# A written-out issue order around the third and fourth head pairs of an attention block: w_out's first half loaded earlier, its folds spread, w_ada's last quarters moved behind the fourth pair's scores

## The chip, the cores and the metric

One Trainium2 chip, one core. The metric is the device time of one execution in microseconds (us); lower is better. The kernel computes one layer of a decoder trunk for 512 tokens of width 1024 in float32.

## The reference, cut to what matters

```python
mod = silu(c) @ w_ada[l] + b_ada[l]                  # 1 x 6144: shift, scale, gate, twice
sh_m, sc_m, gt_m, sh_f, sc_f, gt_f = split(mod, 6)
u = layer_norm(x) * (1.0 + sc_m) + sh_m
proj = u @ w_in                                      # q, k, v, forget gate, xb, gb
attn = forgetting_attention(q, k, v, f_logit + b_f)  # 8 heads x 64, blocks of 128 queries
lru  = rg_lru_branch(xb, gb, ...)                    # 512 channels
mix  = concat([rms_norm(attn, g_attn), rms_norm(lru, g_lru)]) @ w_out
x = layer_norm(ALPHA * x + (1.0 + gt_m) * mix, ln1_g, ln1_b)
u = layer_norm(x) * (1.0 + sc_f) + sh_f
ffn = hierarchical_moe(u, ...)                       # top-1 of 4 groups, top-2 of 4 experts
x = layer_norm(ALPHA * x + (1.0 + gt_f) * ffn, ln2_g, ln2_b)
```

## The kernel before, in words

Float32 products of the large matrices are made from three passes of a short-mantissa type: each operand is split into a high part (a cast on ScalarE, `whi`) and the rest (a subtraction on VectorE, `wlo`), and `mm3` (lines 101 to 103) issues high x high, high x low and low x high. Weights arrive by DMA as raw 512 KB tiles in five buffers of a pool (`raw`, `NRW = 5` on line 219); their split halves have four buffers of each kind (`hilo`, `NHL = 4`). A tile that is asked for takes a buffer that an earlier tile has left, and the DMA that fills it waits, in SyncE's queue, until the last reader of that earlier tile is done. SyncE issues all these transfers in one order, so a transfer that waits holds up all behind it. Matmul results live in eight PSUM banks (`ps`); small working tiles of 2 KB per partition (`t2k`: softmax rows `pr`, their transposes `pt`, sums `part`) have ten buffers.

The work comes in a front part (conditioning, LayerNorm, projections, the RG-LRU branch), a middle part (attention, the output projection, the router's folds) and a last part (LayerNorm, routing, sixteen experts, the final LayerNorm). In the middle part the order of every engine is written by hand: `TAIL` (line 39) returns a list of steps, and line 1580 calls them in turn. On SyncE, TensorE, ScalarE, VectorE and GpSimd the instructions run in exactly that order (line 1072). The steps that matter here:

- `pj(i, n)` (line 1097) projects the queries (n = 0) or the keys (n = 1) of head pair i: 24 matmuls on TensorE, then `qk_evac` (line 662), one operation on ScalarE and one on VectorE. It also calls `w_ahead`, which loads a coming block of `w_in` and splits it; a separate step `w_ahead` stands once in the list.
- `AL` (line 1111) loads one quarter of a 512-column block of `w_ada` (one 512 KB transfer on SyncE). `AC` (line 1115) multiplies it with the conditioning vector on TensorE: every second `AC` issues the eight matmuls of two quarters (line 290), and the fourth of a block has ScalarE copy the sum out and issue a small DMA. `AU[j]` (line 1066) uses the finished block j: eight small matmuls (line 318 or 512) and one VectorE or ScalarE operation.
- `S[m]`, `N[m]`, `T[m]`, `PV[m]` (`att_S`, `att_N`, `att_T`, `att_PV`, lines 836 to 911) are the four stages of attention unit m: scores on TensorE, then the row maximum on VectorE (`nmx`) and the exponentials on ScalarE; division by the row sums on VectorE (`rcs`, `pr`); eight transposes on TensorE (line 883), whose results ScalarE and VectorE split into `pt`; the product with the values on TensorE, and its evacuation (`at`, `sq`). Units 0 to 3 are the four head pairs for the last 128 queries (512 keys), units 4 to 7 those for the third block of queries (384 keys), and so on.
- `LW["L"]` and `LW["A"]` (line 1103) load four 128 x 1024 blocks of `w_out` each; L is the half that multiplies the RG-LRU branch, A the half that multiplies attention. `GW(n, k, V)` (line 742) multiplies block k by the gate row on VectorE. `FW[n][k]` (`fold_wo`, line 745) scales it by a norm gain while it splits it: one operation on ScalarE, one on VectorE. It frees the block's raw buffer and takes a buffer of `hilo`.
- `open_e1` (line 753) gives the space of the projection input (`uh`, `ul`, last read by `pj(3, 1)`) to a new pool and loads the four tiles of x into it. `RW[0]` loads two rows.
- `lo(t, h)` (line 769) is the RG-LRU half of the output projection for 128 tokens and 512 columns: 12 matmuls that need all four folded L blocks. `le(t, h)` adds its result to x on VectorE. `XA[t]` scales x on ScalarE; `scsh_rows` and `FR[...]` (lines 685 to 717) fold scale and shift into the router's weights.

`ACT whi` of line 748 and `DVE wlo` of line 749 in the trace are the two operations of `FW`; `DVE wo` of line 743 is `GW`.

Of the kernel before, what the change touches and what calls it, by code (L numbers as in the profile page):

```python
# [19 lines left out]
S = 512  # L20
# [18 lines left out]
def TAIL(d):  # L39
    (S_, N_, T_, PV_, oh, oe, lo, L, SS, RT, RE, RL, RN, FR, FO, FM, FX, AL, AC, G, V, K, KR, SX, open_e1, open_e3, ahead, pre_split, pj, w_ahead, AU, LW, GW, FW, XA, E5, RW, scsh_rows, R, IX, OR, PT, SP_, PP, WM) = (d[k] for k in ("S_", "N_", "T_", "PV_", "oh", "oe", "lo", "L", "SS", "RT", "RE", "RL", "RN", "FR", "FO", "FM", "FX", "AL", "AC", "G", "V", "K", "KR", "SX", "open_e1", "open_e3", "ahead", "pre_split", "pj", "w_ahead", "AU", "LW", "GW", "FW", "XA", "E5", "RW", "scsh_rows", "R", "IX", "OR", "PT", "SP_", "PP", "WM"))  # L40
    S, N, T, PV, le = S_, N_, T_, PV_, oe
    return [
        AL, AL, pj(1, 0), AC, AC, AL, AL, pj(1, 1), AC, AC, T[0], S[1], N[1], AU[6], AL, AL, pj(2, 0), AC, AC, AL, AL, pj(2, 1), T[1], AC, AC, AL, AL, PV[0], S[2], AU[7], AL, AL, AC, AC, N[2], LW["L"], w_ahead, pj(3, 0), AC, AC, GW("L", 0, V), GW("L", 1, V), FW["L"][0], AU[8], pj(3, 1), FW["L"][1], T[2], GW("L", 2, V), S[3], PV[1], FW["L"][2], N[3], GW("L", 3, V), LW["A"], S[4], T[3], FW["L"][3], open_e1, AU[9], RW[0], N[4], PV[2], PV[3], scsh_rows, FR[0], FR[1], XA[0], XA[2], lo(0, 1), GW("A", 0, V), lo(0, 0), lo(1, 0), FR[2], le(0, 0), XA[1], S[5], T[4], N[5], GW("A", 1, V), S[6], lo(2, 1), PV[4], RW[1], FR[3], FR[4], lo(2, 0), GW("A", 2, V), GW("A", 3, V), le(1, 0), AU[10], lo(1, 1), FR[5], le(0, 1), le(1, 1), XA[3], S[7], T[5], N[6], SS[3], le(2, 1), S[8], PV[5], lo(3, 0), T[6], N[7], le(2, 0), AU[11], lo(3, 1), FW["A"][0], FW["A"][1], FW["A"][2], FW["A"][3], le(3, 0), T[7], E5, N[8], PV[6], S[9], le(3, 1), oh(3, 0), oh(3, 1), T[8], oe(3, 0), PV[7], N[9], S[10], T[9], N[10], PV[8], oe(3, 1), SS[2], oh(2, 1), oh(2, 0), L[3][0], T[10], RT[3], oe(2, 0), RE[3], PV[9], L[3][1], PV[10], RL[3], SS[1], oe(2, 1), open_e3, ahead(4), oh(1, 0), L[3][2], L[2][0], SS[0], RT[2], RE[2], L[3][3], L[2][1], oh(1, 1), oe(1, 0), oe(1, 1), L[2][2], L[1][0], RN[3], L[3][4], oh(0, 0), RT[1], RE[1], L[1][1], L[2][3], oh(0, 1), RL[2], oe(0, 0), oe(0, 1), L[0][0], RT[0], RL[1], L[1][2], RE[0], RN[2], L[1][3], L[0][1], RL[0], L[0][2], K(10), SX[3], RN[1], L[0][3], SX[2], RN[0], ahead(3), R[0], KR("em", 5), R[1], KR("oh1", 5), R[2], R[3], FO, L[2][4], R[4], FM(3), IX[0], OR, FM(2), L[1][4], PT, SP_, FM(1), L[0][4], PP, FM(0), pre_split(0), FX, IX[1], pre_split(1), SX[1], SX[0], WM, pre_split(2), pre_split(3),
    ]


# [1 line left out]
def block_kernel(ctx, tc, x, c, w_ada, b_ada, w_in, b_f, conv_w, conv_b, w_rg, b_rg, w_ig, b_ig,  # L48
# [1531 lines left out]
    for f_ in TAIL(locals()):  # L1580
        f_()
# [297 lines left out]
```

## Time and profile before

| | |
|---|---|
| three timed runs, median (lowest to highest) | 669.8 us (667.96 to 671.28) |
| the profiled execution: device time | 673.18 us |
| its span, first to last instruction | 671.4 us |
| mean granted TensorE clock | 0.955 |
| TensorE matmuls busy | 604.4 us (90%) |
| TensorE weight loads busy | 443.9 us (66%) |
| VectorE busy | 460.7 us (69%) |
| ScalarE busy | 322.5 us (48%) |
| GpSimd busy | 186.4 us (28%) |

All times in the rows are microseconds from the first instruction of that profiled execution, unless a unit is named. The granted clock is a share of TensorE's full speed: 1.00 is 2.4 GHz and 0.50 is 1.2 GHz. Busy time of TensorE is the time in which a matmul was in flight. "idle before <-releaser" is how long an engine stood before an instruction and which instruction's end released it. The steps of the list above cover about 143 us to 325 us of the span.

### The profile page before, as it was taken

How to read it: one execution, taken by the hardware profiler on the slowest of the kernel's cores; microseconds unless marked ns; L12 is line 12 of the kernel's file. 1: busy time of each engine (PE TensorE's matmuls, PEld its weight loads, DVE VectorE, ACT ScalarE, POOL GpSimd, SP SyncE). 2: the span in 40 equal slices, each digit the busy share in tenths (PEclk: the TensorE clock that was granted, in tenths of full speed). 3: DMA queues.
4: the chain of work that ended last, by engine and by line, in shares of the span. 5: the costliest groups of instructions: out<-in, count | busy, mean ns of one | idle time of the engine just before them, and what ended most of it. 6: DMA issues, size and time to landing. Idle time of an engine off the chain costs nothing.

```text
span 671.4 us, 10247 instructions
## 1 busy us (share of the span) xinstructions
PE 604.4 (90%) x3545; PEld 443.9 (66%) x3545; DVE 460.7 (69%) x739; ACT 322.5 (48%) x508; POOL 186.4 (28%) x191
## 2 busy tenths in 40 slices
PE   4698999999977999999889999999999899999960
PEld 0456868767757887978767776576667577676440
DVE  6757779844366559777698576938686885984185
ACT  0334877343244345653376464545445474552070
POOL 8700004000000000041244354425353444443023
PEclk9899999999996999995999999999999999999795
DMA  9996055976535204285599978799989999799502
GB/s 314 339 250 217 3 166 185 292 210 220 188 127 220 95 1 131 91 330 185 208 306 383 381 265 303 281 318 348 357 292 347 369 372 360 265 386 385 189 19 110
DMA packets 90578, 164.61 MB, mean 245 GB/s; under 512 B 9321, under 2 KB 29913, under 8 KB 90524
## 3 DMA queue, kind: packets, MB, share of 16 engines
q1 hardware_dynamic: 83796, 149.02, 63.6%
q0 software_dynamic: 5024, 10.70, 6.0%
q10 hardware_dynamic: 1704, 4.21, 1.7%
q8 instruction: 29, 0.48, 0.3%
q14 instruction: 25, 0.20, 0.1%
HBM read 155.54 MB, written 12.39 MB: 250 GB/s over the span
## 4 chain that ended last, share of the span: by engine, by line
PE 66%; DVE 12%; DMA 9%; ACT 6%; issue 4%; POOL 2%; ACTq 0%; SPq 0%; DVEq 0%; POOLq 0%
PE ps L101 12%; PE ps L102 12%; PE ps L103 12%; PE ps L1418 9%; DMA wa<-in_w_ada_dram 4%; PE ps L1434 3%; DVE wlo L812 3%; DMA er<-in_w_e_down_dram 2%; DMA wi<-in_w_in_dram 2%; PE ps L290 2%; DVE tail L1753 1%; PE ps L883 1%; DMA er<-in_w_e_gate_dram 1%; PE ps L318 1%; ACT pr L861 1%
## 5 line engine op out<-in xcount | busy, mean ns | idle before, releaser
L812 DVE TENSOR_TENSOR wlo<-er,whi 128x1024 fp32r<-128x1024 f32 x91 | 148.5, 1650 | 29.4 <-ACT whi L811 29.4
L811 ACT CAST whi<-er 128x1024 fp32r<-128x1024 f32 x120 | 125.2, 1049 | 71.3 <-PE ps L103 66.1
L812 POOL TENSOR_TENSOR wlo<-er,whi 128x1024 fp32r<-128x1024 f32 x29 | 74.0, 2553 | 78.1 <-ACT whi L811 77.8
L101 PE MATMUL ps<-uh,whi 128*128 128x512 f32 x160 | 64.5, 403 | 0.0
L103 PE MATMUL ps<-uh,wlo 128*128 128x512 f32 x160 | 62.6, 391 | 0.0
L102 PE MATMUL ps<-ul,whi 128*128 128x512 f32 x160 | 62.5, 391 | 0.0
L102 PE MATMUL ps<-wlo,xth 128*128 128x512 f32 x144 | 57.8, 401 | 5.0 <-POOL wlo L812 3.7
L1418 PE MATMUL ps<-er,xT 128*64 128x256 f32 x512 | 61.1, 393 | 0.0
L101 PE MATMUL ps<-whi,xth 128*128 128x512 f32 x144 | 59.0, 410 | 0.0
L103 PE MATMUL ps<-whi,xtl 128*128 128x512 f32 x144 | 57.7, 401 | 1.2 <-DVE xtl L98 1.2
L1418 PEld LDWEIGHTS ps<-er,xT 128*64 128x64 f32 x512 | 36.4, 141 | 21.9 <-issue 6.4
L326 POOL TENSOR_TENSOR rA<-rA,nhalf 128x1 f32<-128x1 f32 x4 | 2.2, 551 | 168.2 <-DVE rA L917 168.2
L101 PEld LDWEIGHTS ps<-uh,whi 128*128 128x128 f32 x160 | 30.1, 188 | 12.7 <-issue 3.0
L358 DVE TENSOR_TENSOR wlo<-wi,whi 128x1024 fp32r<-128x1024 f32 x20 | 25.5, 1275 | 17.6 <-ACT whi L357 17.6
L102 PEld LDWEIGHTS ps<-wlo,xth 128*128 128x128 f32 x144 | 27.6, 192 | 12.6 <-POOL wlo L812 5.4
L357 ACT CAST whi<-wi 128x1024 fp32r<-128x1024 f32 x20 | 21.0, 1048 | 30.9 <-DMA wi<-in_w_in_dram 22.5
L103 PEld LDWEIGHTS ps<-uh,wlo 128*128 128x128 f32 x160 | 30.0, 188 | 6.9 <-DVE wlo L358 0.5
L102 PEld LDWEIGHTS ps<-ul,whi 128*128 128x128 f32 x160 | 30.1, 188 | 6.4 <-issue 0.5
L102 PE MATMUL ps<-wlo,hth 128*128 128x512 f32 x80 | 31.9, 399 | 2.6 <-DVE wlo L812 2.6
L103 PEld LDWEIGHTS ps<-whi,xtl 128*128 128x128 f32 x144 | 27.5, 191 | 7.9 <-DVE xtl L98 1.6
L101 PE MATMUL ps<-whi,hth 128*128 128x512 f32 x80 | 32.4, 405 | 0.0
L103 PE MATMUL ps<-whi,htl 128*128 128x512 f32 x80 | 31.6, 395 | 0.0
(416 smaller groups left out, 1266.7 us busy)
## 6 DMA issues: line engine op xcount, KB each, us to landing
er<-in_w_e_gate_dram SPq DMA_DIRECT2D x64, 512.0 KB, 10.4
er<-in_w_e_up_dram SPq DMA_DIRECT2D x64, 512.0 KB, 10.6
er<-in_w_e_down_dram SPq DMA_DIRECT2D x64, 512.0 KB, 11.5
wa<-in_w_ada_dram SPq DMA_DIRECT2D x44, 512.0 KB, 6.3
wi<-in_w_in_dram SPq DMA_DIRECT2D x20, 512.0 KB, 6.4
wo<-in_w_out_dram SPq DMA_DIRECT2D x8, 512.0 KB, 3.7
wa<-in_w_ada_dram ACTq DMA_DIRECT2D x4, 512.0 KB, 3.9
x<-in_x_dram SPq DMA_DIRECT2D x4, 512.0 KB, 7.1
```

Of the source, the lines that this page charges most:

```text
L101: T.matmul(o, l[0], r[0], start=start, stop=False)
L102: T.matmul(o, l[0], r[1], start=False, stop=False)
L103: T.matmul(o, l[1], r[0], start=False, stop=stop)
L290: T.matmul(part_p[j][32 * k:32 * k + 32, :], cb[:, 2 * kh - 2 + k, :], part_q[j][kh - 1 + k // 2][:, k % 2, :], start=kh == 1, stop=kh == 3)
L318: T.matmul(p[:, b:b + 1], part[:, b * 128:(b + 1) * 128], s4 if sel_ is None else sel_, start=True, stop=True)
L357: A.copy(hl[0], r)
L358: V.tensor_sub(hl[1], r, hl[0].bitcast(F32))
L811: A.copy(hl[0], r)
L812: (eng or V).tensor_sub(hl[1], r, hl[0].bitcast(F32))
L861: A.activation(pr[j][:, n, :], lg_[j][:, n, :], AF.Exp, bias=nmx[:, j, n:n + 1], accum_out=ss[:, j, n:n + 1])
L1418: T.matmul(p[64 * h:64 * h + 64, :], xT[:, k, :], ws[w0 + k // 2][:, k % 2, h * 256:(h + 1) * 256], start=k == 0, stop=k == 7)
L1434: T.matmul(py[64 * h:64 * h + 64, :], hT[:, k % 2, (k // 2) * 64:(k // 2) * 64 + 64], ws[8 + k][:, h * 512:(h + 1) * 512], start=k == 0, s ...
```

## The change

Only the list in `TAIL` changes, and only its first hundred steps. The same functions are called, and the same work is done, in another order; the step `w_ahead` is dropped. Written one stretch to a line:

```diff
   AL, AL, pj(1, 0), AC, AC, AL, AL, pj(1, 1), AC, AC, T[0], S[1], N[1], AU[6],
-  AL, AL, pj(2, 0), AC, AC, AL, AL, pj(2, 1), T[1], AC, AC, AL, AL, PV[0], S[2], AU[7],
-  AL, AL, AC, AC, N[2], LW["L"], w_ahead, pj(3, 0), AC, AC,
-  GW("L", 0, V), GW("L", 1, V), FW["L"][0], AU[8], pj(3, 1), FW["L"][1], T[2], GW("L", 2, V),
-  S[3], PV[1], FW["L"][2], N[3], GW("L", 3, V), LW["A"], S[4], T[3], FW["L"][3], open_e1,
-  AU[9], RW[0], N[4], PV[2], PV[3], scsh_rows, FR[0], FR[1], XA[0], XA[2], lo(0, 1),
-  GW("A", 0, V), lo(0, 0), lo(1, 0), FR[2], le(0, 0), XA[1],
+  pj(2, 0), LW["L"], AL, GW("L", 0, V), GW("L", 1, V), FW["L"][0], pj(2, 1), AL, T[1], PV[0],
+  S[2], AU[7], N[2], AC, AC, FW["L"][1], GW("L", 2, V), AL, pj(3, 0), AU[8], FW["L"][2],
+  GW("L", 3, V), AL, pj(3, 1), AC, AC, AU[9], open_e1, T[2], S[3], N[3], PV[1], S[4],
+  FW["L"][3], AL, AL, AL, AL, PV[2], T[3], N[4], RW[0], lo(0, 1), AC, AC, PV[3], LW["A"],
+  scsh_rows, FR[0], FR[1], XA[0], XA[2], lo(0, 0), AC, AC, GW("A", 0, V), lo(1, 0), FR[2],
+  le(0, 0), le(0, 1), XA[1],
   S[5], T[4], N[5], GW("A", 1, V), S[6], lo(2, 1), PV[4], RW[1],
...
-  AU[10], lo(1, 1), FR[5], le(0, 1), le(1, 1), XA[3], S[7], T[5],
+  AU[10], lo(1, 1), FR[5], le(1, 1), XA[3], S[7], T[5],
...
```

The twelve `AL` and twelve `AC` of the list are the quarters of blocks 9, 10 and 11 of `w_ada`. In both lists block 9 is done first, unchanged. Block 10's products (two pairs of `AC`) and block 11's move: before, one pair each stood behind `pj(2, 0)`, `T[1]`, `AU[7]` and `pj(3, 0)`; after, they stand behind `N[2]`, `pj(3, 1)`, `lo(0, 1)` and `lo(0, 0)`.

## Rows read from the trace of the kernel before

**Rows 1.** Busy time by stretch: us, PE, PEld, DVE, ACT, POOL, PEclk, DMA share, GB/s.
```profile
197.60:205.10 7.50, 0.03 (x2) 0.03 (x1) 4.27 (x9) 3.54 (x9) 0.00 (x0) 0.75 0.08 32
205.10:211.60 6.50, 6.50 (x30) 6.29 (x31) 3.38 (x6) 3.12 (x7) 0.00 (x0) 0.50 0.94 339
211.60:224.00 12.40, 11.94 (x69) 10.15 (x68) 5.61 (x14) 5.56 (x13) 0.00 (x0) 1.00 0.63 232
224.00:250.00 26.00, 26.00 (x178) 22.14 (x178) 17.27 (x36) 10.39 (x33) 0.55 (x1) 1.00 0.02 8
```

**Rows 2.** What TensorE waited for, 130 to 275 us: total, times, longest.
```profile
PE ps L883 <- DVE pr L871: 9.0, 3, 7.5
```

**Rows 3.** Timeline of TensorE around the pause: start, us, line, operands, count.
```profile
197.26 0.35 PE L856 MATMUL ps<-mnh,idh 64*128 64x128 f32 x4
205.07 2.15 PE L883 MATMUL ps<-ident,pr 128*128 128x128 f32 x8 [7.47 <-DVE pr L871]
```

**Rows 4.** Timeline of VectorE, 195 to 206 us.
```profile
196.35 0.69 DVE L98 TENSOR_TENSOR pt<-ps,pt 128x512 fp32r<-128x512 f32 x1 [0.16 <-ACT pt L97]
196.96 1.22 DVE L743 TENSOR_TENSOR wo<-wo,gtm 128x1024 f32<-128x1024 f32 x1
198.09 1.28 DVE L858 TENSOR_REDUCE nmx<-ps 128x1 f32<-128x512 f32 x2
200.76 0.59 DVE L908 TENSOR_TENSOR at<-ps,at 64x128 fp32r<-64x128 f32 x2 [1.40 <-ACT at L905]
203.13 1.28 DVE L749 SCALAR_TENSOR_TENSOR wlo<-wo,vt,whi 128x1024 fp32r<-128x1024 f32 x1 [1.78 <-ACT whi L748]
...
204.53 0.88 DVE L871 TENSOR_SCALAR pr<-pr,rcs 128x512 f32<-128x512 f32 x2
```

**Rows 5.** Timeline of TensorE through one unit's steps at full clock, 165 to 179 us.
```profile
165.85 1.06 PE L290 MATMUL ps<-wa,cb 128*32 128x512 f32 x8
166.85 0.50 PE L101 MATMUL ps<-uh,whi 128*128 128x512 f32 x1
...
172.43 1.04 PE L883 MATMUL ps<-ident,pr 128*128 128x128 f32 x8
...
174.39 0.39 PE L101 MATMUL ps<-pt,v 128*128 128x256 f32 x1
...
176.01 0.53 PE L851 MATMUL ps<-ncum,sel 64*128 64x512 f32 x2
...
177.34 1.05 PE L318 MATMUL ps<-ones,part 128*128 128x1 f32 x8
178.33 1.06 PE L290 MATMUL ps<-wa,cb 128*32 128x512 f32 x8
```

**Rows 6.** Timeline of VectorE: softmax of unit 2, then gate and first fold of w_out.
```profile
179.94 0.88 DVE L871 TENSOR_SCALAR pr<-pr,rcs 128x512 f32<-128x512 f32 x2
185.73 0.69 DVE L666 SCALAR_TENSOR_TENSOR qk<-ps,qk 128x512 fp32r<-128x512 f32 x1 [4.90 <-ACT qk L665]
186.34 2.35 DVE L743 TENSOR_TENSOR wo<-wo,gtm 128x1024 f32<-128x1024 f32 x2
189.16 1.29 DVE L749 SCALAR_TENSOR_TENSOR wlo<-wo,vt,whi 128x1024 fp32r<-128x1024 f32 x1 [0.47 <-ACT whi L748]
```

**Rows 7.** Timeline of SyncE's queue, 150 to 210 us: start, time to the last issue.
```profile
156.35 0.37 SPq L355 DMA_DIRECT2D wi<-in_w_in_dram  x1
157.05 17.81 SPq L252 DMA_DIRECT2D wa<-in_w_ada_dram  x6
174.95 29.82 SPq L738 DMA_DIRECT2D wo<-in_w_out_dram  x8
204.87 1.81 SPq L759 DMA_DIRECT2D xt<-in_x_dram  x4
```

**Rows 8.** DMA issues, 115 to 290 us: count, KB each, median us to landing.
```profile
wa<-in_w_ada_dram SPq DMA_DIRECT2D x20, 512.0 KB, 5.0
...
wo<-in_w_out_dram SPq DMA_DIRECT2D x8, 512.0 KB, 3.7
```

**Rows 9.** Busy time by stretch around two short pauses of TensorE, columns as in rows 1.
```profile
267.00:268.00 1.00, 0.00 (x0) 0.00 (x0) 0.92 (x5) 0.53 (x2) 0.00 (x0) 1.00 0.00 0
...
350.00:352.00 2.00, 0.79 (x3) 0.49 (x2) 2.00 (x4) 0.00 (x0) 0.00 (x0) 0.89 1.07 282
352.00:354.00 2.00, 2.00 (x6) 1.52 (x6) 2.00 (x10) 0.39 (x1) 1.18 (x2) 0.50 1.03 361
```

## The prediction made before the change was run

> **What bounds the kernel now.** I read the busy shares first (TensorE is the busiest engine), then TensorE's waits in the middle part, then the windows around the longest one, then the timelines of the engines that it waited for. In the middle part TensorE is full except at one place. It stands 9.0 us for the division of the softmax rows, 7.5 of them at once [rows 2]: unit 4's scores end at 197.6, and unit 3's transposes begin at 205.07 after 7.47 us of waiting [rows 3]. The granted clock falls in that pause, from 1.00 (2.4 GHz) to 0.50 (1.2 GHz), and stays there until about 211.6: 6.50 us of work at half speed [rows 1], which at full clock is 3.25. In the next window TensorE stands another 0.46 (12.40 less 11.94) [rows 1]. The stretch loses 7.47 + 3.25 + 0.46 = 11.2 us. From 224 to 250 TensorE is busy all of the time and the DMA engines almost none [rows 1], so what starts there waits for TensorE and not for data: time won before 224 moves all that follows, the expert loads included, which wait for buffers that this work frees.
>
> The reason for the pause is on VectorE [rows 4]. In the old list `T[3]` is the next TensorE step and needs unit 3's rows, but ahead of the division stand a gate multiplication (1.22), the row maxima (1.28), a wait for the exponentials, the evacuation of `PV[1]` (0.59), and a fold (1.28) that itself waited 1.78 for its half on ScalarE. Nothing independent is left on TensorE; both projections of the fourth pair and all w_ada products have been spent.
>
> **The change part by part.** *TensorE.* Nothing is added or removed; the steps are the same. Prices at full clock, from starts that follow each other [rows 5]: a pair of `AC` 1.0 (165.85 to 166.85), a `pj` 5.6 (to 172.43), transposes 1.0, `PV` 1.6 (174.39 to 176.01), `S` 1.3, `AU` 1.0; `lo`, 12 products of the form of `pj`'s 24, 2.8. Until 165.85, the end of `pj(2, 0)`, both lists agree on TensorE. Laid end to end in the new order: `pj(2, 1)` to 171.4, `T[1]` 172.4, `PV[0]` 174.0, `S[2]` 175.3, `AU[7]` 176.3, block 10's first products 177.3, `pj(3, 0)` 182.9, `AU[8]` 183.9, `pj(3, 1)` 189.5, block 10's last products 190.5, `AU[9]` 191.5, `T[2]` 192.5, `S[3]` 193.8, `PV[1]` 195.4, `S[4]` 196.7, `PV[2]` 198.3, `T[3]` 199.3, `lo(0, 1)` 202.1. Now each step's inputs.
>
> *The pause itself.* Undisturbed, a unit's scores that end at 177.34 [rows 5] have their rows divided at 179.94 + 0.88 = 180.8 [rows 6], 3.5 us later. `S[3]` ends at 193.8, so the rows are there at 197.3, and `T[3]` asks at 198.3. `PV[1]`, `S[4]` and `PV[2]` are the cover, 4.5 us, against 3.5 needed; without `PV[2]` 0.6 would show. No gate or fold stands between any more. The 7.47 goes, and with it the slow clock and the 0.46, which stood behind the same queues: 11.2.
>
> *w_out's first half.* The four loads now stand before block 10's quarters in SyncE's queue. Their buffers are left by blocks whose release let transfers go at 156.35 and 157.05 [rows 7], so I put their issue at 151 to 158 and the landing, 3.7 later [rows 8], by 162. The gates stand on VectorE behind the evacuation of `pj(2, 0)`; rows 6 show that sequence later in the old list: 0.61 from evacuation to gate, then 4.1 (186.34 to 190.45) for two gates and a fold. It ends at about 171.4, and VectorE is free when `pj(2, 1)` wants to be evacuated; `S[2]` needs that result at 174.0, with about 1.2 to spare. `FW["L"][1]` and `[2]` fall beside `pj(3, 0)` and `pj(3, 1)`, when VectorE is mostly idle (4.90 us before the evacuation at 185.73 [rows 6]). These cost nothing; without `pj` beside them each would cost its 2.5 or so.
>
> *w_ada's quarters.* The second quarter of block 10 takes the buffer that `FW["L"][0]` leaves at 171.4; landing takes 3.7 to 5.0 [rows 8], so it is there between 175.1 and 176.4. Its product asks at 176.8 (the second half of the pair): 0.4 to 1.7 to spare, cost 0, at worst under 1. Block 11's four quarters now stand behind `open_e1`'s four x loads, which wait for `pj(3, 1)`, 189.5. The sixth of these transfers, 3.1 MB, lands 9.3 us later at the 339 GB/s of 205 to 211 us, 13.6 at 232 [rows 1], that is 199 to 203; `AC` asks at 202 to 203. Cost 0, at worst 1. The x loads themselves were late before (204.87, behind the fourth fold's buffer [rows 7]) and come early now. `LW["A"]` is passed by the quarters and by `RW[0]`; its fourth block can only take the buffer of block 11's last products, about 212, but its gate stands behind two more score blocks, so this is free. ScalarE's two small DMAs go with their copies, GpSimd has no instruction among the moved steps, and the dropped `w_ahead` is empty, since all twenty blocks are loaded by then.
>
> *Two new waits.* `FW["L"][3]` stands behind `S[4]`'s exponentials on ScalarE, and `lo(0, 1)` now comes right after `T[3]`. VectorE: rows of unit 3 divided 197.3, `PV[1]`'s subtractions 0.6 [rows 4] to 197.9, `S[4]`'s maxima and exponentials up to 2.6 (177.34 to 179.94) but shorter with 384 columns, to about 200.3; the fold 1.2 on ScalarE and 1.3 on VectorE: 202.8. `lo(0, 1)` asks for the fourth block after nine products, 201.5: a wait of about 1.3. Queued behind it on VectorE are `PV[2]`'s evacuation (0.6) and the two halves of `pt` of unit 3 (0.69 each [rows 4]), to about 205.5; `PV[3]` asks for the second at 203.4 + 1.0 + 0.8 = 205.2. With the first half also late I take 0.6. Together 1.9; bounds 0 (ScalarE and VectorE each 2 us ahead of this) and 4. The early `le(0, 1)` adds 0.7 to VectorE before `S[5]`'s maxima and takes it away later; TensorE has three steps in front of both, so 0.
>
> **Sum:** 11.2 - 1.9 = 9.3 us. On the profiled execution's own 673.2: 663.9. That execution was 3.4 slower than the median of the runs, so on the median: 669.8 - 9.3 = 660.5.
>
> **Rivals.** *The clock falls at the new waits.* A pause of 1.2 us before 352 was followed by a clock of 0.50, while one of a whole microsecond, 267 to 268, left it at 1.00 [rows 9]. Two waits within 5 us could bring it down over `lo(0, 1)`, `PV[3]` and the router's small products. For 3 to 10 us of half-speed work the loss is 1.5 to 5: 662 to 665.5. The Trainium skill ("TensorE: Matmul & The Clock Gate", section "A second HAM failure mode: psum-queue depth-cycling") says that short idle spells between groups of matmuls are enough to make the clock swing. Of the two pauses in rows 9 one agrees with that and one doesn't.
>
> *Data comes late.* SyncE's order makes block 10's second quarter or block 11's first ones miss their products by 1 to 4 us. Rows 7 and 8 speak against it by under 2 us of slack each: 661 to 665.
>
> *The change doesn't do what it says; the pause only moves.* If ScalarE or VectorE is some 6 us behind at `FW["L"][3]`, TensorE stands before `lo(0, 1)` as long as it stood before `T[3]`, with the slow clock after it: 667 to 671. Against it: the fourth pair's projections now cover the folds.
>
> *Slower.* The gates of `w_out` stand on VectorE ahead of `pj(2, 1)`'s evacuation, and in-order engines take a late load over in full. If blocks 0 and 1 land later than 169.7 (168.5 when the gate asks, plus 1.2 of slack), TensorE stands before `S[2]` for each microsecond more; from 179 on the win is spent, and at 184 the time is about 675. That needs the loads to be issued after 175, as in the old list (174.95 [rows 7]), because their buffers come free only with later products. The releases at 156.35 and 157.05 speak against it.
>
> **How the numbers follow.** Forecast 0.70; clock 0.11; data 0.07; moved pause 0.07; slower 0.05. About 0.5% (3.3 us) is what a measurement of this kernel can tell from no change. Nearly all of the first three is a win of more than that: faster 0.86; same 0.09; slower 0.05. Low end: no new waits, 658.6, less the 1.8 by which the runs fall below their median, 656.8. High end: the clock or data cases at 665.5, plus 1: 666.5.
>
> **What would show it.** Right: no wait over 2 us before `T[3]`; a clock of 1.00 from 190 to 225; `S[5]`'s scores start near 215 in place of 224; a wait of about 1 us before `lo(0, 1)`, on `wlo` of line 749, and a shorter one before `PV[3]`; no wait of `AC` for its data; the `wo` loads issued before 160. Wrong: a pause of several us before `lo(0, 1)`, `AC` or `S[2]`, a slow clock behind it, or a later start of the experts' loads that takes the win back.

## The result, and the profile after

The changed kernel takes 660.7 us (median of 4 runs, 657.28 to 666.39) against 670.54 for the kernel before in the same set: a ratio of 0.9853, 95% interval 0.9805 to 0.9902. A second set of runs gave 662.49 against 672.15, ratio 0.9858, interval 0.9812 to 0.9905. The forecast was 660.5, range 656.8 to 666.5, faster.

The profiled execution's span fell from 671.4 to 660.6. What TensorE waits for in the changed stretch, 150 to 225 us (total, times, longest), in the kernel after:

```profile
PE ps L102 <- DVE wlo L749: 0.8, 1, 0.8
PE ps L102 <- DVE pt L98: 0.3, 1, 0.3
```

The wait of 7.47 us for `pr` in [rows 2, 3] is gone from this stretch, and two waits that the kernel before didn't have stand there instead. TensorE's timeline around them in the kernel after (start, us, line, operands; in brackets the idle time before and its releaser):

```profile
195.46 1.04 PE L883 MATMUL ps<-ident,pr 128*128 128x128 f32 x8
...
198.19 0.40 PE L103 MATMUL ps<-whi,ml 128*128 128x512 f32 x1
198.47 0.49 PE L101 MATMUL ps<-whi,mh 128*128 128x512 f32 x1
199.79 0.50 PE L102 MATMUL ps<-wlo,mh 128*128 128x512 f32 x1 [0.83 <-DVE wlo L749]
...
200.44 1.06 PE L290 MATMUL ps<-wa,cb 128*32 128x512 f32 x8
201.49 0.38 PE L101 MATMUL ps<-pt,v 128*128 128x256 f32 x1
202.21 0.39 PE L102 MATMUL ps<-pt,v 128*128 128x256 f32 x1 [0.34 <-DVE pt L98]
```

`T[3]` (line 883) has no bracket: it waits for nothing. `lo(0, 1)` gets through nine products and one more, then stands for the fourth folded block; `PV[3]` stands for the split of its transposes. VectorE over the same time, which answers to [rows 4]:

```profile
194.14 0.88 DVE L871 TENSOR_SCALAR pr<-pr,rcs 128x512 f32<-128x512 f32 x2
194.94 0.58 DVE L908 TENSOR_TENSOR at<-ps,at 64x128 fp32r<-64x128 f32 x2
195.55 1.02 DVE L858 TENSOR_REDUCE nmx<-ps 128x1 f32<-128x384 f32 x2
198.45 1.28 DVE L749 SCALAR_TENSOR_TENSOR wlo<-wo,vt,whi 128x1024 fp32r<-128x1024 f32 x1 [1.88 <-ACT whi L748]
199.65 0.58 DVE L908 TENSOR_TENSOR at<-ps,at 64x128 fp32r<-64x128 f32 x2
201.47 1.29 DVE L98 TENSOR_TENSOR pt<-ps,pt 128x512 fp32r<-128x512 f32 x2 [1.23 <-ACT pt L97]
```

The division of unit 3's rows (194.14) comes before the only fold that is left here, where in [rows 4] one gate and one fold stood ahead of it. The second wait hangs on the same fold, by way of ScalarE: its half of the split of `pt` stands behind the square of `PV[2]`'s result (`sq`), and that waits for VectorE, which evacuates `PV[2]` only after the fold:

```profile
200.27 0.56 ACT L911 ACTIVATE sq<-ps 64x128 f32<-64x128 f32 x2 [1.44 <-DVE at L908]
200.85 1.08 ACT L97 CAST pt<-ps 128x512 fp32r<-128x512 f32 x2
```

The windows of the kernel after that answer to [rows 1] (us, PE, PEld, DVE, ACT, POOL, PEclk, DMA share, GB/s):

```profile
195.00:204.00 9.00, 7.83 (x51) 5.45 (x49) 5.41 (x13) 5.01 (x14) 0.00 (x0) 1.00 1.02 390
204.00:212.50 8.50, 8.50 (x49) 6.31 (x48) 2.57 (x6) 4.80 (x9) 0.00 (x0) 1.00 0.51 180
212.50:238.50 26.00, 26.00 (x180) 22.20 (x180) 17.29 (x36) 10.74 (x35) 0.55 (x1) 1.00 0.17 59
```

TensorE stands 1.17 us of the 9.00 and the clock stays at 1.00 (2.4 GHz). From 212.5 on it is full again, as in the last of [rows 1].

A measure that the runs below share: **D**, from the start of `AU[6]`'s products (line 318) to the start of unit 5's scores (line 851). Between the two lie all the moved TensorE steps, and nothing else that changed on TensorE. In the kernel before:

```profile
159.27 0.94 PE L318 MATMUL ps<-ones,part 128*128 128x1 f32 x7
...
223.97 0.44 PE L851 MATMUL ps<-ncum,sel 64*128 64x384 f32 x2
```

and in the kernel after:

```profile
157.31 0.83 PE L318 MATMUL ps<-ones,part 128*128 128x1 f32 x6
...
212.53 0.44 PE L851 MATMUL ps<-ncum,sel 64*128 64x384 f32 x2
```

D is 64.70 before and 55.22 after, a win of 9.48. Of the 10.8 us between the two spans, another 1.96 had come before the first changed step of TensorE, and 0.64 went back behind the last (447.4 us from unit 5's scores to the end before, 448.1 after). TensorE's instructions are the same in both places. The 1.96 isn't put down to the change: in the table below `AU[6]` starts between 158.17 and 159.27 in the old order and between 157.08 and 159.23 in the new one.

All profiled executions of this study by that measure, worked out from the same two rows of each:

| kernel | `AU[6]` starts | D | rest of the span | `T[3]` starts after `AU[6]` |
|---|---|---|---|---|
| before | 159.27 | 64.70 | 447.4 | 45.8 |
| after | 157.31 | 55.22 | 448.1 | 38.2 |
| after, second profile | 158.29 | 55.21 | 443.9 | 38.1 |
| order only | 158.17 | 61.49 | 446.1 | 40.7 |
| folds back | 158.91 | 62.21 | 447.8 | 44.1 |
| last fold early | 158.81 | 53.32 | 447.7 | 38.2 |
| no cover | 158.03 | 54.54 | 449.4 | 37.4 |
| filler in the kernel before | 158.49 | 64.79 | 442.3 | 45.9 |
| block 10 back | 158.71 | 55.15 | 441.8 | 38.3 |
| all folds ahead | 159.23 | 63.72 | 446.3 | 46.6 |
| all folds ahead, filler | 157.08 | 62.67 | 444.3 | 46.7 |

D came out within 0.01 us in the two profiled executions of the changed kernel, the only one that was profiled twice. The rest of the span, the same TensorE instructions in all, varies by 7.6. So single times don't rank these kernels, and the experiments are read by D, one execution each.

### The profile page after: what moved, and what is told of

Same layout as the page of the kernel before. It is cut to its first block, busy times and chain, and to the rows that moved or that the text cites. A ratio compares the mean times of both kernels' runs of the same rounds, so it can differ in the third digit from the quotient of the medians.

```text
span 660.6 us, 10240 instructions
## 1 busy us (share of the span) xinstructions
PE 601.3 (91%) x3545; PEld 442.5 (67%) x3545; DVE 459.8 (70%) x739; ACT 322.5 (49%) x508; POOL 187.7 (28%) x191
## 5 line engine op out<-in xcount | busy, mean ns | idle before, releaser
L812 DVE TENSOR_TENSOR wlo<-er,whi 128x1024 fp32r<-128x1024 f32 x91 | 145.1, 1612 | 31.6 <-ACT whi L811 30.0
L101 PEld LDWEIGHTS ps<-whi,xth 128*128 128x128 f32 x144 | 27.9, 194 | 5.8
```

Of the source, the lines that this page charges most:

```text
L101: T.matmul(o, l[0], r[0], start=start, stop=False)
L812: (eng or V).tensor_sub(hl[1], r, hl[0].bitcast(F32))
```

## The experiments

**Order only.** Is it the queue on VectorE, or the early loads and the moved products? The kernel before, with unit 3's division brought ahead of the last two gates and folds. TensorE and SyncE keep their orders; only VectorE's and ScalarE's change:

```diff
-T[2], GW("L", 2, V), S[3], PV[1], FW["L"][2], N[3], GW("L", 3, V), LW["A"], S[4], T[3],
-FW["L"][3], open_e1, AU[9], RW[0], N[4], PV[2], PV[3], scsh_rows
+T[2], S[3], N[3], PV[1], S[4], T[3], AU[9], GW("L", 2, V), FW["L"][2], GW("L", 3, V), LW["A"],
+FW["L"][3], PV[2], PV[3], open_e1, RW[0], N[4], scsh_rows
```

> The kernel before with one reordering: unit 3's division, PV[1], unit 4's scores, T[3] and AU[9] come ahead of the last two gates and folds of w_out's first half, and PV[2], PV[3] behind them. Loads and w_ada's products stay where they were. Measure: D, from the start of AU[6]'s matmuls to the start of unit 5's scores, which took 64.7 us before and 55.2 after. Queue theory (the pause came from gates and folds ahead of the division on VectorE): the wait before T[3] falls from 7.5 to 2 or 3 us, but the folds now end late, so lo(0, 1) waits 2 to 4 us; D 58.5 to 61. Rival (the early loads and the moved products are what gave the time): D stays at 64 or above.

TensorE's waits, 150 to 222 us, and the windows (columns as above):

```profile
PE ps L883 <- DVE pr L871: 2.4, 1, 2.4
PE ps L101 <- ACT whi L748: 1.2, 1, 1.2
PE ps L102 <- DVE wlo L749: 0.8, 1, 0.8
```

```profile
196.40:198.90 2.50, 0.08 (x2) 0.00 (x0) 1.42 (x5) 1.85 (x6) 0.00 (x0) 0.93 0.29 113
198.90:205.20 6.30, 6.29 (x29) 6.08 (x30) 2.54 (x6) 2.95 (x8) 0.00 (x0) 0.50 0.00 0
...
210.00:212.00 2.00, 0.82 (x5) 0.36 (x3) 0.78 (x2) 1.22 (x2) 0.00 (x0) 1.00 0.62 166
212.00:214.00 2.00, 1.18 (x4) 0.78 (x5) 1.74 (x3) 0.56 (x3) 0.00 (x0) 1.00 1.01 391
214.00:216.00 2.00, 2.00 (x11) 1.60 (x10) 0.99 (x4) 1.28 (x6) 0.00 (x0) 1.00 0.97 391
```

The wait before `T[3]` fell from 7.5 to 2.4 and the folds, now late, held `lo(0, 1)` for 2.0, as the queue theory said. D is 61.49, half a microsecond outside what was expected. The expectation had no slow clock in it, but even the wait of 2.4 brought the clock down to 0.50 (1.2 GHz) for 6.3 us; the 2.00 us of waits from 210 to 214 did not. Reordering VectorE and ScalarE alone is worth 3.2 of the 9.5, since the gates and folds still have to be done somewhere. Whether they could have been done beside the fourth pair's projections with the loads in their old place, no run shows: the four blocks were issued between 173.8 and 185.0 here, and `pj(3, 1)` ended at 191.3.

**Folds back.** The other way round: the changed kernel, loads and products where the change put them, with two folds and two gates put ahead of unit 3's division. That is one of each more than the kernel before had between unit 2's `pt` and the division [rows 4].

```diff
-N[2], AC, AC, FW["L"][1], GW("L", 2, V), AL, pj(3, 0), AU[8], FW["L"][2], GW("L", 3, V), AL, pj(3, 1)
+N[2], AC, AC, AL, pj(3, 0), AU[8], AL, pj(3, 1)
...
-T[2], S[3], N[3], PV[1]
+T[2], S[3], FW["L"][1], GW("L", 2, V), FW["L"][2], GW("L", 3, V), N[3], PV[1]
```

> The changed kernel with FW L1, GW L2, FW L2, GW L3 put back between unit 3's scores and its division; loads and w_ada's products stay moved. Queue theory: VectorE has 5 us of gates and folds and two waits for ScalarE ahead of the division, so T[3] waits 5 to 7 us again, the clock falls to 0.50 behind it, D 62 to 66 where the changed kernel has 55.2. Rival (early loads and moved products carry the win): D stays below 57.

The timeline of VectorE in this kernel, from unit 3's maxima to its division:

```profile
192.98 1.28 DVE L858 TENSOR_REDUCE nmx<-ps 128x1 f32<-128x512 f32 x2
196.27 1.29 DVE L749 SCALAR_TENSOR_TENSOR wlo<-wo,vt,whi 128x1024 fp32r<-128x1024 f32 x1 [2.01 <-ACT whi L748]
197.47 1.22 DVE L743 TENSOR_TENSOR wo<-wo,gtm 128x1024 f32<-128x1024 f32 x1
199.91 1.28 DVE L749 SCALAR_TENSOR_TENSOR wlo<-wo,vt,whi 128x1024 fp32r<-128x1024 f32 x1 [1.22 <-ACT whi L748]
201.11 1.22 DVE L743 TENSOR_TENSOR wo<-wo,gtm 128x1024 f32<-128x1024 f32 x1
202.24 0.16 DVE L868 RECIPROCAL rcs<-ss 128x2 f32<-128x2 f32 x1
202.51 0.88 DVE L871 TENSOR_SCALAR pr<-pr,rcs 128x512 f32<-128x512 f32 x2
```

and TensorE's answer, with the window behind it:

```profile
203.05 2.15 PE L883 MATMUL ps<-ident,pr 128*128 128x128 f32 x8 [5.86 <-DVE pr L871]
```

```profile
203.00:209.00 6.00, 5.95 (x18) 4.87 (x19) 3.67 (x8) 3.57 (x11) 0.00 (x0) 0.50 0.64 249
```

The pause is back (5.86), the slow clock too, and D is 62.21. Early loads and moved products are worth 2.5 of the 9.5 while this many folds stand ahead of the division.

**Block 10 back.** Is the early load of `w_out` needed as early as the change has it? The changed kernel with block 10 of `w_ada` loaded and multiplied at its old places, and `w_out`'s half loaded behind `AU[7]`:

```diff
-AU[6], pj(2, 0), LW["L"], AL, GW("L", 0, V), GW("L", 1, V), FW["L"][0], pj(2, 1), AL, T[1], PV[0],
-S[2], AU[7], N[2], AC, AC, FW["L"][1], GW("L", 2, V), AL, pj(3, 0), AU[8], FW["L"][2],
-GW("L", 3, V), AL, pj(3, 1), AC, AC, AU[9]
+AU[6], AL, AL, pj(2, 0), AC, AC, AL, AL, pj(2, 1), T[1], AC, AC, PV[0], S[2], AU[7], LW["L"],
+N[2], GW("L", 0, V), GW("L", 1, V), FW["L"][0], pj(3, 0), FW["L"][1], GW("L", 2, V), AU[8],
+FW["L"][2], GW("L", 3, V), pj(3, 1), AU[9]
```

> The changed kernel with block 10's loads and products of w_ada back at their old places, and w_out's first half loaded only behind them (behind AU[7]) and folded beside the fourth pair's projections; block 11 stays behind unit 4's scores. Theory: buffers and landings still leave the folds beside the projections, TensorE's steps are the same, D 55.0 to 56.0: loading w_out behind the third pair's queries is not needed for the win. Rival (the early load is needed): the gates wait for their data, the evacuations behind them on VectorE are late, D 57 to 64.

D is 55.15, the changed kernel's within 0.1. The queue of SyncE in this kernel (start, time to the last issue):

```profile
156.45 0.88 SPq L252 DMA_DIRECT2D wa<-in_w_ada_dram  x2
163.38 10.85 SPq L738 DMA_DIRECT2D wo<-in_w_out_dram  x4
189.81 1.75 SPq L759 DMA_DIRECT2D xt<-in_x_dram  x4
```

The four blocks are issued between 163 and 174, where the change issues them between 149 and 156, and TensorE's only waits are the same two. The load has to be there when the fourth pair's projections run, not when the third's do, and block 10's move isn't needed either. Block 11 stays moved in this kernel; no run puts its quarters back ahead of the load, so whether that part is needed isn't shown.

**No cover.** The changed kernel with `PV[2]` behind `T[3]`:

```diff
-AL, AL, AL, AL, PV[2], T[3], N[4]
+AL, AL, AL, AL, T[3], PV[2], N[4]
```

> The changed kernel with PV[2] put behind T[3], so that the cover of unit 3's softmax is 1.6 us shorter. The prediction said that without PV[2] a wait of 0.6 us would show before T[3]. Theory: a wait of 0.6 to 1.3 us there, and about as much less before lo(0, 1), whose last fold ends at its own time; D 55.0 to 55.9. Rival (the waits add up): D 56.3 to 57.

```profile
195.47 1.29 PE L883 MATMUL ps<-ident,pr 128*128 128x128 f32 x8 [0.77 <-DVE pr L871]
```

This is the one wait in its stretch (TensorE's timeline). The cover is worth what was said, 0.77 where the prediction had 0.6, but D is 54.54, lower than the 55.0 to 55.9 expected and lower than the changed kernel's. `PV[2]` now stands before `lo(0, 1)`, where it covers the wait for the last fold and, with `T[3]` done earlier, the one for `pt` as well: neither shows any more. The same 1.6 us of work cover more there.

**The last fold early.** What are the two new waits worth?

```diff
-AL, pj(3, 1), AC, AC, AU[9]
+AL, pj(3, 1), FW["L"][3], AC, AC, AU[9]
...
-S[4], FW["L"][3], AL, AL, AL, AL
+S[4], AL, AL, AL, AL
```

> The changed kernel with FW L3 moved ahead of unit 3's softmax, right behind pj(3, 1). If the two new waits (0.8 before the last products of lo(0, 1), 0.3 in PV[3]) come from this fold's place behind unit 4's exponentials, both go and D falls from 55.2 to 53.8 to 54.5, about 1 us of the total, which timing can hardly tell. Rival: the fold delays unit 3's softmax on VectorE and ScalarE and T[3] waits instead, D 55 to 57.

TensorE waits for nothing between 150 and 225 us, and D is 53.32, 1.90 under the changed kernel's and below the 53.8 to 54.5 expected. The waits are more than their idle time: a product that follows another starts 0.23 later, so the gap from 198.47 to 199.79 above lost 1.1 and not 0.83. Timed: 659.05 us (654.51 to 661.59), ratio to before 0.9807, interval 0.9758 to 0.9855. That is a lower median than the changed kernel's in the same set (662.49), but the intervals overlap, so that it beats the change is shown by D and not by the times.

> The changed kernel itself, for the interval and beside the variant with the last fold early on the same chip. Theory: 0.985 to 0.987 of before, D 55.2 within 0.3. Rival (part of the first measurement was spread between executions): ratio above 0.99, D unchanged.

Measured: 0.9858, D 55.21.

**Filler in the kernel before.** Was the slow clock a cost of its own? Thirty extra small products (60 matmuls in the trace), results unused, ahead of `T[3]`:

```diff
-LW["A"], S[4], T[3], FW["L"][3]
+LW["A"], S[4], K(30), T[3], FW["L"][3]
```

> The kernel before with 30 extra small matmuls (128 x 128, results unused) ahead of T[3], which fill most of the pause of 7.47 us. They shorten nothing; if the clock fell because TensorE stood, it now stays at 1.00, T[3] still starts about 46 us after AU[6], and only the half-speed loss goes: D 61.3 to 62.0 in place of 64.7. Rival (the lower clock is not due to the pause): D 64 to 65.

Windows, columns as above:

```profile
196.70:203.60 6.90, 6.90 (x63) 6.77 (x60) 3.72 (x7) 3.54 (x9) 0.00 (x0) 1.00 0.10 39
203.60:212.50 8.90, 6.97 (x55) 6.12 (x53) 7.10 (x16) 3.67 (x10) 0.00 (x0) 1.00 0.88 330
212.50:216.20 3.70, 3.70 (x14) 3.10 (x14) 2.52 (x6) 2.56 (x8) 0.00 (x0) 0.56 0.51 204
```

The filler held the clock at 1.00 through the old pause, and `T[3]` started at its old place. D is 64.79: nothing won. Where the loss went shows in the start of `lo(0, 1)`, in the kernel before:

```profile
215.30 0.48 PE L101 MATMUL ps<-whi,mh 128*128 128x512 f32 x1
```

and, behind `T[3]`, with filler:

```profile
204.38 1.29 PE L883 MATMUL ps<-ident,pr 128*128 128x128 f32 x8 [0.66 <-DVE pr L871]
...
213.14 0.77 PE L101 MATMUL ps<-whi,mh 128*128 128x512 f32 x1
```

Counted from `T[3]` (205.07 before [rows 3]), `lo(0, 1)` starts after 10.23 us before and after 8.76 with filler: 1.47 of the estimated 3.25 was won by then. The rest wasn't, since at full speed TensorE ran into the queue on ScalarE and VectorE: of the 1.93 us that it stands in the 8.90, 0.66 lies ahead of `T[3]` and 1.27 behind it, where the kernel before stood 0.46. Then the clock fell after all, and `lo(0, 1)` at half speed lost the 1.47 again: unit 5's scores start 18.90 after `T[3]` in both. So the 0 is no price of the clock; it wasn't kept up to the end. Neither theory had said that.

**All folds ahead, without and with filler.** To see the clock's price where no queue stands behind `T[3]`, the changed kernel with all the late folds ahead of the division, and the same with 34 small products, results unused:

```diff
-T[2], S[3], N[3], PV[1], S[4], FW["L"][3], AL, AL, AL, AL, PV[2], T[3]
+T[2], S[3], FW["L"][1], GW("L", 2, V), FW["L"][2], GW("L", 3, V), FW["L"][3], N[3], PV[1], S[4],
+AL, AL, AL, AL, PV[2], T[3]            # second kernel: PV[2], K(34), T[3]
```

(`FW["L"][1]`, `GW("L", 2, V)`, `FW["L"][2]` and `GW("L", 3, V)` are gone from their places beside `pj(3, 0)`, as in the kernel with the folds back.)

> The changed kernel with FW L1, GW L2, FW L2, GW L3 and also FW L3 between unit 3's scores and its division. Nothing is left that could keep TensorE waiting behind T[3] (the variant with the last fold early had no wait there and D 53.3). Theory: T[3] starts 46 to 47 us after AU[6] in place of 38.2, a pause of about 8.5 us, and the clock at 0.50 behind it costs 3 more: D 64.5 to 65.5. Rival (the slow clock costs nothing of its own): D 61.5 to 62.3.

> The same with 34 extra small matmuls (128 x 128, results unused) ahead of T[3], which fill most of that pause. Theory: T[3] starts at the same place, the clock stays at 1.00, and since no queue stands behind T[3] the half-speed loss now really goes: D 61.5 to 62.5, some 3 us under the kernel without filler. Rival (as with the filler in the kernel before, other waits take the loss over): D within 1 us of the kernel without filler.

Windows without filler, then with it:

```profile
197.50:205.80 8.30, 0.01 (x1) 0.00 (x0) 5.76 (x8) 2.70 (x4) 0.00 (x0) 0.82 0.73 246
205.80:209.40 3.60, 3.53 (x12) 3.03 (x13) 2.29 (x8) 2.18 (x8) 0.00 (x0) 0.50 0.79 286
```

```profile
195.20:203.70 8.50, 7.75 (x70) 7.56 (x68) 5.96 (x8) 2.71 (x4) 0.00 (x0) 1.00 0.70 244
203.70:207.20 3.50, 3.41 (x18) 2.82 (x19) 2.19 (x7) 2.18 (x8) 0.00 (x0) 1.00 0.84 272
```

The pause was sized well (8.4 measured, 8.5 expected), the clock was not: it was back at 1.00 at 209.6, after some 3.7 us of work and not 6.5, so D came out at 63.72, under the expected 64.5. Beside the kernel with the last fold early, which waits for nothing, the price can be read off: `T[3]` starts 8.49 later, and 63.72 - 53.32 - 8.49 leaves 1.91 lost behind it, half of the slow 3.7 within 0.1. The kernel with the folds back adds up in the same way: `T[3]` 5.99 later, 2.90 lost behind it, 5.9 us at 0.50. So the rival of the first kernel, that the slow clock costs nothing of its own, failed too.

With the clock held up D is 62.67, 1.05 less than without filler, and not 1.91: the transposes of `T[3]` took longer than at full speed in the changed kernel (1.38 us for 1.04), and a wait for `pt` in `PV[3]` took part back:

```profile
203.73 1.38 PE L883 MATMUL ps<-ident,pr 128*128 128x128 f32 x8 [0.77 <-DVE pr L871]
...
209.43 0.39 PE L102 MATMUL ps<-pt,v 128*128 128x256 f32 x1 [0.22 <-DVE pt L98]
```

The expectation of 3 was wrong, and the rival, that it stays within 1 us, all but held.

## Why the prediction was right, and where it wasn't

**The pause.** The step that carried the forecast held as worked out: the division is late because of gates and folds in VectorE's order, and with these elsewhere the rows are ready before `T[3]` asks. Put there again, they bring the pause back (folds back); moved behind `T[3]`, they bring part of it back elsewhere (order only). The margin was thinner than forecast: the rows were divided at 195.02 and `T[3]` started at 195.46, 0.4 to spare in place of 1.0, and without `PV[2]` 0.77 showed in place of 0.6.

**The total of 11.2.** The stretch without any wait takes 53.32 (last fold early), so the kernel before lost 64.70 - 53.32 = 11.4 in it. The sum of 11.2 was right as a balance. **The term for the clock, 3.25,** had the right kind of size: where nothing waits behind the pause, half of the slow time is what was lost (2.90 and 1.91). But it isn't a gain that stands by itself. With the clock held up through the pause, 1.05 of the 1.91 came back, and slower transposes and a wait for `pt` took the rest; in the kernel before nothing came back, because of such waits and because the clock fell later. The change got this term because it removed the queue and with it the pause in which the clock fell. Of the 11.4 it won 9.48; the rest are the new waits.

**The new waits, 1.9.** Named at their places, `FW["L"][3]` behind unit 4's exponentials and then the `pt` of unit 3; measured 55.22 - 53.32 = 1.90. The parts were cut a little differently: 1.1 and 0.5 by starts for the forecast's 1.3 and 0.6, the rest in smaller gaps beside them. That the second part fits owes something to luck. The forecast's own terms for it, 202.8 + 0.6 + 2 x 0.69, give 204.8 and not 205.5, which is before the 205.2 at which `PV[3]` was to ask, and the path was another: `PV[3]` waited for the first half of `pt`, and VectorE itself stood 1.23 us there for ScalarE.

**Loads.** The `wo` blocks were issued from 148.9 to 155.9, 2 earlier than forecast in an execution that ran 1.96 earlier; x at 187.1 (189.5 forecast); no product of w_ada waited. **The slack of 1.2 before `S[2]`** was 0.9: the evacuation of `pj(2, 1)` ended at 170.75 and the scores began at 171.63. `LW["A"]` and its fourth block cost nothing that shows.

**The rival of the clock** didn't happen to the changed kernel: two waits within 5 us left it at 1.00. It is a real case all the same: in the kernel with filler short waits brought it down, and in order only one of 2.4, while 2.00 us of waits within 4 left it up there. The forecast gave it 0.11, without a rule that tells these apart; none of these runs gives one. **Slower by late loads** was not near: with the loads 14 us later (block 10 back) D is the same.

**The number.** 660.5 against 660.7 owes something to luck. The win in the stretch was sized to 0.2 us, but the same TensorE instructions behind it take from 441.8 to 449.4 us from one execution to the next.

## What to carry to other kernels

When a full engine stops at one place, look at what stands ahead of the awaited instruction on the engine that it waits for, and move that under work that leaves this engine idle; moving loads matters only so far as it makes that possible. A loss seen as slow clock isn't a gain to be had in full by itself (1.05 of 1.91 here): ask what would be waited for next at full speed. Where executions scatter by more than the change, measure the changed stretch between two instructions that both kernels share.

## What the runs showed of the hardware that was not expected

After a pause the clock stayed at 0.50 for different lengths of work: 6.5 us in the kernel before [rows 1], 6.3 in order only, 5.9 in folds back and some 3.7 in all folds ahead. What followed the pause doesn't explain that: in the last two it is the same, transposes and `lo(0, 1)`. They differ in when the clock fell: at about 202.1 in folds back, 0.9 before `T[3]`, and at about 202.8 in all folds ahead, 3.1 before `T[3]`. Slow clock inside the pause cost nothing: `T[3]` starts 46.6 us after `AU[6]` there, and 46.7 with the clock held up. The clock fell after one pause of 2.4 us (order only) and after 1.93 us of short waits within 8.9 (filler), and did not fall after 1.17 within 9.0 (the kernel after) or 2.00 within 4 (order only). So the sum of the idle time doesn't tell these cases apart, and no run here shows what does. The part behind the changed stretch varies by 7.6 us between executions of the same TensorE instructions; what sets it was not looked into.
